# The factors of a chunked scan, queued run by run behind the splits of weights

## Chip, cores and metric

The kernel runs on one core of one Trainium2 chip. The metric is the device time of one execution in microseconds, of which the median over several runs is taken; smaller is better. A profile of one execution comes beside it, with the time at which every instruction of every engine started and ended. The engines are TensorE (PE in the profile; PEld is its weight load), VectorE (DVE), ScalarE (ACT), GpSimd (POOL) and SyncE (SP), which issues most DMAs.

## What is computed

One layer of a streaming encoder for 288 tokens: 256 of a new stream and 32 of a running one, with all values in float32. The change lies in the state-space mixer, whose scan is, per chunk:

```python
xc = (xh * dt[..., None]).reshape(b, c, q, G, J, P)
acum = jnp.cumsum(a, axis=-1)
diff = acum[..., :, None] - acum[..., None, :]
lmat = jnp.exp(jnp.where(causal, diff, -jnp.inf))
cb = jnp.einsum('bclgn,bcsgn->bcgls', Cc, Bc)
y_diag = jnp.einsum('bcgls,bcgjls,bcsgjp->bclgjp', cb, lmat, xc)
...
y_off = jnp.einsum('bclgn,bcgjpn,bcgjl->bclgjp', Cc, h_prev, jnp.exp(acum))
y = (y_diag + y_off).reshape(b, s, G, J, P) + D[..., None] * xh
```

There are 32 heads of 64 channels. Around the scan stand the projections `proj = xn @ w_in` (2048 to 5664 columns), a pooling mixer, an output projection and a feed-forward block with a depthwise convolution.

## The kernel before

**Products in three parts.** Each float32 product is made of three matmuls. A piece of weights (128 x 1024) is split: ScalarE copies it to a rounded high part `whi` (L137 in `split_w`), VectorE subtracts to get the low part `wlo` (L138), and TensorE multiplies high by high, high by low and low by high (L144 to L146). Each of `raw`, `whi` and `wlo` has four buffers. A `project` is 256 columns of an output, 16 tiles deep: four pieces, 24 matmuls each, into two accumulators `acc`.

**The mixer's loop.** After the first columns, seven projects make the channels `xs` (scan numbers 1 to 7) and eight make the gate `z` (numbers 8 to 15). Behind each project VectorE moves its two accumulators out of PSUM: for a gate that is `z = acc * rstd` (L555, twice), whose last instruction is kept in `last_in[0]`. Then `scan(i)` is called.

**The scan.** The heads are treated in eight fours, q0 to q7. `four_in(q)` loads a four's decays `gb`, its state `h0t` and its channels `xw` through SP, and makes its factors. On ScalarE that is an exponential for `ce` and one for `elast`, twelve Relu (L496) and one exponential over 128 x 1664 values of `m` (L499). On VectorE it is three products: `ce` (L489), `xw` (L492) and `m` (L501). `gb`, `h0t`, `xw`, `ce` and `m` have two buffers each. `four_out` is the use: 16 small matmuls into `py` a four (L523), then VectorE adds the result to `xs`. `four_in` is called in the scans of `SCAN_IN = {5, 6, 7, 8, 9, 11, 12, 13}`, `four_out` for the two fours that are ready in those of `SCAN_OUT = {7, 9, 12, 14}`, at its start. So the scans 7, 9, 12 and 14 let out q0 and q1, q2 and q3, q4 and q5, q6 and q7.

**The order of work.** Each engine runs its own queue in order. Where an instruction stands in a queue is set by a scheduler that works ahead of the run; the code leads it by priorities (`tc.high_priority`; the evacuations and the splits go ahead of what is written before them), by `tc.keep_in_program_order`, and by `tc.issue_after(x)`, which puts an instruction in its engine's order behind `x`. In `four_in` all factors stand under `tc.issue_after(last_in[0].ins)`.

Of the kernel before, what the change touches and what calls it, by code (L numbers as in the profile page):

```python
# [10 lines left out]
AF = mybir.ActivationFunctionType  # L11
# [32 lines left out]
def body(  # L44
# [24 lines left out]
    act, dve, pool, pe, sp = nc.scalar, nc.vector, nc.gpsimd, nc.tensor, nc.sync  # L69
# [11 lines left out]
    def aux(shape, name):  # L81
        return aux_ps.tile(shape, F32, tag="aux", name=name)
# [7 lines left out]
    def halves(t):  # L90
        return t.rearrange("p (r j) -> p r j", r=2)
# [20 lines left out]
    def wtile(part, n, nc_):  # L112

        t = wpool.tile([P, 1024 + 64], F32R, tag=part, name="w" + part)
        return t[:, 58 : 58 + n * nc_].rearrange("p (k c) -> p k c", k=n)

    ahead = [0]

    def fetch_w(view, kb, nk, c0, nc_):
        raw = wpool.tile([P, nk, nc_], F32, tag="raw", name="raw")  # L120
        with tc.high_priority(offset=ahead[0]):
            sp.dma_start(out=raw, in_=view[:, c0 // 256, kb : kb + nk, :nc_])
        return raw

    def split_w(raw, kb, nk, nc_, after=()):

        out = []
        step = min(nk, 1024 // nc_)
        for k in range(0, nk, step):
            n = min(step, nk - k)  # L130
            hi = wtile("hi", n, nc_)
            lo = wtile("lo", n, nc_)
            with ExitStack() as order:
                order.enter_context(tc.high_priority(offset=ahead[0]))
                for ins in after:
                    order.enter_context(tc.issue_after(ins.ins))
                act.activation(hi, raw[:, k : k + n, :], AF.Copy)  # L137
                dve.tensor_tensor(lo, raw[:, k : k + n, :], hi.bitcast(F32), op=ALU.subtract)  # L138
            out.append([(kb + k + i, hi[:, i, :], lo[:, i, :]) for i in range(n)])
        return out  # L140
# [123 lines left out]
    for kb, n in chunks:  # L264
        raw = wpool.tile([P, n, 768], F32, tag="raw", name="raw")
# [19 lines left out]
        for k in range(kb, kb + n):  # L285
# [11 lines left out]
            hi, lo = wtile("hi", 1, 768)[:, 0, :], wtile("lo", 1, 768)[:, 0, :]  # L297
# [20 lines left out]
    for r in range(4):  # L318
        for q in range(4):
            k = 4 * q + r  # L320
# [28 lines left out]
    last_in = [None]  # L349
# [123 lines left out]
    def four_in(q):  # L473

        c = slice(2 * P * q, 2 * P * q + 2 * P)
        gb = mp.tile([P, 4, MW], F32, tag="gb", bufs=2, name="gb")
        sp.dma_start(out=gb, in_=g_d[4 * q : 4 * q + 4, :].unsqueeze(0).broadcast_to([P, 4, MW]))
        h0t = mp.tile([P, 2 * P], F32, tag="h0t", bufs=2, name="h0t")
        sp.dma_start(out=h0t, in_=state_ssd[:, c])
        xw = mp.tile([P, 3, 2 * P], F32, tag="xw", bufs=2, name="xw")  # L480
        sp.dma_start(out=xw[:, 0:2, :], in_=xs_d[:NP_, c].rearrange("(b p) c -> p b c", p=P))
        sp.dma_start(out=xw[:, 2, :], in_=xs_d[NT - P :, c])
        ce = mp.tile([P, 4, NS], F32, tag="ce", bufs=2, name="ce")
        m = mp.tile([P, 4, MW], F32, tag="m", bufs=2, name="m")
        with tc.issue_after(last_in[0].ins):
            act.activation(ce, gb[:, :, 384:], AF.Exp)
            act.activation(elast[:, 4 * q : 4 * q + 4], gb[:, :, MW - 1], AF.Exp)
            cs = bc[2 + q // 4][:, NP_:]
            dve.tensor_tensor(ce, ce, cs.unsqueeze(1).broadcast_to([P, 4, NS]), op=ALU.mult)  # L489
            w = tok[:, :, 1, 4 * q : 4 * q + 4].unsqueeze(3).broadcast_to([P, 3, 4, 64])  # L490
            x4 = xw.rearrange("p b (r q) -> p b r q", r=4)
            dve.tensor_tensor(x4, x4, w, op=ALU.mult)  # L492
            for j in range(4):
                h = 4 * q + j
                for b, (lo_, hi_) in enumerate(((0, 256), (256, 384), (384, MW))):
                    act.activation(  # L496
                        m[:, j, lo_:hi_], gb[:, j, lo_:hi_], AF.Relu, bias=tok[:, b, 0, h : h + 1], scale=-1.0
                    )
            act.activation(m, m, AF.Exp, scale=-1.0)  # L499
            gi = q // 4  # L500
            got = dve.tensor_tensor(m, m, cbt[:, gi : gi + 1, :].broadcast_to([P, 4, MW]), op=ALU.mult)  # L501
        return xw, h0t, ce, m, got

    def four_out(q, ys, xw, h0t, ce, m, _, after=None):

        ops = []
        for k in range(4):
            for j in range(4):
                c = slice(64 * j, 64 * j + 64)
                y = ys[j // 2][64 * (j % 2) : 64 * (j % 2) + 64, :]  # L510
                if k == 0:
                    ops.append((y[:, 0:256], xw[:, 0, c], m[:, j, 0:256], True, False))
                elif k == 1:
                    ops.append((y[:, 128:256], xw[:, 1, c], m[:, j, 256:384], False, True))
                elif k == 2:
                    ops.append((y[:, 256:], xw[:, 2, c], m[:, j, 384:], True, False))
                else:
                    ops.append((y[:, 256:], h0t[:, c], ce[:, j, :], False, True))
        for y, w_, v_, go, end in ops:
            with ExitStack() as order:  # L520
                if after is not None:
                    order.enter_context(tc.issue_after(after.ins))
                ins = pe.matmul(y, w_, v_, start=go, stop=end)  # L523
            tc.keep_in_program_order(ins)
            after = None
        for i in range(2):
            t = 2 * q + i
            dve.scalar_tensor_tensor(xs[t], xs[t], dcol[:, t : t + 1], ys[i], op0=ALU.mult, op1=ALU.add)

    def gate_rstd(t, pin=False):  # L530
        p_ = aux([P, NT], "psum_g")
        ins = pe.matmul(p_, mean, gsum[t], start=True, stop=True)
        if pin:
            tc.keep_in_program_order(ins)
        o = const.tile([P, NT], F32, tag="spread", bufs=3, name="rg")
        root(o, p_, 0.5)
        return o
# [42 lines left out]
    fours = list(range(NX // 2))  # L580
    gates = list(range(NX))
    done = [-1]
    ready = []
    rg = []

    def scan(i):
        if i in SCAN_OUT:
            ys = [aux([P, NT], "py") for _ in range(3)] + [acc_ps.tile([P, NT], F32, tag="acc", name="py_a")]
            for n, (q, got) in enumerate(ready):
                four_out(q, ys[2 * n : 2 * n + 2], *got, after=None if n else ready[-1][1][-1])  # L590
            done[0] = 2 * ready[-1][0] + 1
            ready.clear()
        if i == 13:
            assert gates[0] >= 8
            rg.append(gate_rstd(0, True))
        if i in SCAN_IN:
            q = fours.pop(0)
            assert 2 * q + 1 < len(xs)
            ready.append((q, four_in(q)))

    def run_gates():
        while gates and gates[0] in zs and gates[0] <= done[0]:
# [2 lines left out]
    for i in range(1, NX // 2):  # L605
        ps = project(win, [(O_X + 256 * i, 256)], xn, K16)
        xs_evac(i, ps)
        xs_conv(i - 1)
        scan(i)
# [189 lines left out]
    def state_in(x, apart=False):  # L799

        if apart:
            room = [state_slot() for _ in range(5)]
            hi, lo = (room[3], room[4], room[0]), room[1:3]
        else:
            hi = stp[0].tile([P, 3, 512], F32R, tag="shi", name="shi")
            lo = stp[0].tile([P, 2, 512], F32R, tag="slo", name="slo")
        if apart:
            for b in (2, 0, 1):
                act.activation(hi[b], x[b], AF.Copy)
                q = top if b == 2 else slice(0, P)  # L810
                o = hi[2] if b == 2 else lo[b]
                dve.tensor_tensor(o[q], x[b][q], hi[b][q].bitcast(F32), op=ALU.subtract)
        else:
            act.activation(hi, x, AF.Copy)
            dve.tensor_tensor(hi[top, 2, :], x[top, 2, :], hi[top, 2, :].bitcast(F32), op=ALU.subtract)
            dve.tensor_tensor(lo, x[:, 0:2, :], hi[:, 0:2, :].bitcast(F32), op=ALU.subtract)
            hi, lo = ([t[:, b, :] for b in range(t.shape[1])] for t in (hi, lo))
        return hi, lo
# [41 lines left out]
    for grp in ((0, 1), (2,), (3,), (4,), (5,), (6,), (7,)):  # L860
# [5 lines left out]
        if grp[0] == 2:  # L866
            j = grp[0] // 2 - 1
            x = state_load(j)
            hi, lo = state_in(x)
# [49 lines left out]
    for k in range(KD):  # L919
        if k % 2 == 0:  # L920
            raw = wpool.tile([P, 2, 896], F32, tag="raw", name="raw")
# [4 lines left out]
        hi = act.activation(halves(a[:, 0, :]), src, AF.Copy, scale=g_ffn_pre[:, k : k + 1])  # L926
# [10 lines left out]
        else:  # L937
            q = out_temp()
# [217 lines left out]
    for kb, n in ((0, K_RUN), (K_RUN, 8), (K_RUN + 8, 8)):  # L1156
        raw = fetch_w(wd2, kb, n, (KD - 2) * P, 256)
# [141 lines left out]
```

## Time and profile before

| | |
|---|---|
| median of 3 runs | 1233.65 us (1233.14 to 1234.08) |
| profiled execution | 1235.27 us, of which the span of its instructions is 1233.0 |
| TensorE busy | 1225.3 us, 99% of the span |
| VectorE busy | 888.2 us, 72% |
| ScalarE busy | 670.2 us, 54% |
| mixer with its scan | about 86 to 240 us of the span |
| let out of the scans 7, 9, 12, 14 | about 131, 158.6, 197.7 and 226.2 us |

A row of the timeline gives the start in us, the duration, the engine, the line of the code, the operation with what it writes and reads, and in brackets an idle time ahead of it with what ended that. A row of groups gives the count, the busy time, the mean length in ns, and the idle time ahead with its releaser. A row of waits tells which instruction waited for which: microseconds in all, times, longest. In windows each row is a stretch of time with the busy time of each engine, the granted clock of TensorE (1.00 is full), the busy share of the DMA engines and the GB/s.

### The profile page before, as it was taken

How to read it: one execution, taken by the hardware profiler on the slowest of the kernel's cores; microseconds unless marked ns; L12 is line 12 of the kernel's file. 1: busy time of each engine (PE TensorE's matmuls, PEld its weight loads, DVE VectorE, ACT ScalarE, POOL GpSimd, SP SyncE). 2: the span in 40 equal slices, each digit the busy share in tenths (PEclk: the TensorE clock that was granted, in tenths of full speed). 3: DMA queues.
4: the chain of work that ended last, by engine and by line, in shares of the span. 5: the costliest groups of instructions: out<-in, count | busy, mean ns of one | idle time of the engine just before them, and what ended most of it. 6: DMA issues, size and time to landing. Idle time of an engine off the chain costs nothing.

```text
span 1233.0 us, 25222 instructions
## 1 busy us (share of the span) xinstructions
PE 1225.3 (99%) x10059; PEld 1213.7 (98%) x10059; DVE 888.2 (72%) x1484; ACT 670.2 (54%) x1011; POOL 276.3 (22%) x427
## 2 busy tenths in 40 slices
PE   9999999999999999999999999999999999999998
PEld 9999999999999999999999999999999999999997
DVE  8899998989664599887776744446777777765555
ACT  8557787546554466645554544334555454554443
POOL 6395442131341200221211200001112121101110
PEclk9999999999999999999999999999999999999999
DMA  9668785466576555676655455555555555576763
GB/s 356 197 208 307 263 279 172 149 243 221 199 242 216 191 177 201 200 228 181 208 185 171 166 185 179 169 191 188 189 172 175 188 184 172 175 252 198 217 190 118
DMA packets 87589, 249.82 MB, mean 203 GB/s; under 512 B 45712, under 2 KB 51920, under 8 KB 65200
## 3 DMA queue, kind: packets, MB, share of 16 engines
q1 hardware_dynamic: 83184, 240.78, 58.3%
q0 software_dynamic: 3712, 6.95, 1.9%
q8 instruction: 78, 1.28, 0.4%
q10 hardware_dynamic: 576, 0.49, 0.1%
q14 instruction: 39, 0.32, 0.1%
HBM read 236.23 MB, written 11.95 MB: 201 GB/s over the span
## 4 chain that ended last, share of the span: by engine, by line
PE 63%; DMA 1%; DVE 1%; ACT 0%; issue 0%; DVEq 0%
PE acc L144 20%; PE acc L145 20%; PE acc L146 20%; DMA st<-xs_d 1%; PE acc_x L145 0%; PE acc_x L144 0%; PE acc_x L146 0%; PE run_a L1172 0%; PE low L1170 0%; PE run_b L1185 0%; DVE rm L247 0%; PE low L146 0%; PE low L145 0%; PE low L144 0%; DVE sh L836 0%; PE y_ps L1215 0%
## 5 line engine op out<-in xcount | busy, mean ns | idle before, releaser
L138 DVE TENSOR_TENSOR wlo<-raw,whi 128x1024 fp32r<-128x1024 f32 (+1 forms) x386 | 461.3, 1198 | 245.6 <-ACT whi L137 245.3
L137 ACT ACTIVATE whi<-raw 128x1024 fp32r<-128x1024 f32 (+1 forms) x386 | 396.9, 1031 | 349.2 <-PE acc L145 283.4
L145 PE MATMUL acc<-hn,whi 128*128 128x288 f32 x1360 | 382.9, 286 | 0.0
L146 PE MATMUL acc<-hn,wlo 128*128 128x288 f32 x1360 | 382.7, 286 | 0.0
L144 PE MATMUL acc<-hn,whi 128*128 128x288 f32 x1360 | 382.2, 286 | 0.3 <-ACT hn L926 0.3
L144 PEld LDWEIGHTS acc<-hn,whi 128*128 128x128 f32 x1360 | 254.2, 189 | 0.8 <-ACT hn L926 0.7
L145 PEld LDWEIGHTS acc<-hn,whi 128*128 128x128 f32 x1360 | 254.7, 189 | 0.1
L146 PEld LDWEIGHTS acc<-hn,wlo 128*128 128x128 f32 x1360 | 254.6, 189 | 0.0
L144 PE MATMUL acc<-xn,whi 128*128 128x288 f32 x686 | 197.2, 289 | 0.0
L145 PE MATMUL acc<-xn,whi 128*128 128x288 f32 x686 | 195.6, 287 | 0.0
L146 PE MATMUL acc<-xn,wlo 128*128 128x288 f32 x686 | 192.3, 287 | 0.6 <-DVE wlo L138 0.6
L144 PE MATMUL acc<-fa,whi 128*128 128x288 f32 x660 | 188.8, 286 | 0.0
L145 PE MATMUL acc<-fa,whi 128*128 128x288 f32 x660 | 188.8, 286 | 0.0
L146 PE MATMUL acc<-fa,wlo 128*128 128x288 f32 x660 | 188.8, 286 | 0.0
L980 POOL COPY fc_stage<-ebuf 128x4 f32<-128x4 f32 x88 | 28.7, 326 | 463.4 <-DVE ebuf L979 401.2
L144 PEld LDWEIGHTS acc<-xn,whi 128*128 128x128 f32 x686 | 130.1, 190 | 1.4 <-issue 0.9
L145 PEld LDWEIGHTS acc<-xn,whi 128*128 128x128 f32 x686 | 130.1, 190 | 0.3
L146 PEld LDWEIGHTS acc<-xn,wlo 128*128 128x128 f32 x686 | 128.3, 190 | 1.0 <-DVE wlo L138 1.0
L144 PEld LDWEIGHTS acc<-fa,whi 128*128 128x128 f32 x660 | 124.7, 189 | 0.0
L145 PEld LDWEIGHTS acc<-fa,whi 128*128 128x128 f32 x660 | 124.7, 189 | 0.0
L146 PEld LDWEIGHTS acc<-fa,wlo 128*128 128x128 f32 x660 | 124.7, 189 | 0.0
L984 ACT ACTIVATE fc<-ebuf,pf 128x290 f32<-128x290 f32 x88 | 54.4, 622 | 78.7 <-DVE ebuf L979 78.7
(312 smaller groups left out, 1799.8 us busy)
## 6 DMA issues: line engine op xcount, KB each, us to landing
raw<-in_w_up SPq DMA_DIRECT2D x80, 1024.0 KB, 4.8
raw<-in_w_in SPq DMA_DIRECT2D x38, 1024.0 KB, 5.1
raw<-in_w_down SPq DMA_DIRECT2D x32, 1024.0 KB, 4.8
raw<-in_w_out SPq DMA_DIRECT2D x23, 1024.0 KB, 5.1
raw<-in_w_down SPq DMA_DIRECT2D x16, 768.0 KB, 4.5
raw<-in_w_up SPq DMA_DIRECT2D x8, 896.0 KB, 4.7
gb<-g_d SPq DMA_DIRECT2D x8, 832.0 KB, 6.6
raw<-in_w_first SPq DMA_DIRECT2D x5, 768.0 KB, 8.5
```

The source lines that it names most:

```text
L137: act.activation(hi, raw[:, k : k + n, :], AF.Copy)
L138: dve.tensor_tensor(lo, raw[:, k : k + n, :], hi.bitcast(F32), op=ALU.subtract)
L144: pe.matmul(out, wh, hi, start=start, stop=False)
L145: pe.matmul(out, wh, lo, start=False, stop=False)
L146: pe.matmul(out, wl, hi, start=False, stop=stop)
L980: pool.tensor_copy(fc_stage[:, :, :, i], e[:, 256:324].rearrange("p (s c) -> p s c", c=34)[:, :, 0:2])
L984: act.activation(c, e[:, 0:290], AF.Identity, bias=pf[:, 3, i : i + 1], scale=pf[:, 0, i : i + 1])
```

## The change

`four_in` now only loads, and returns its tiles. The factors stand in a new function, `four_mul`, under one more `issue_after`: behind the split `after` of a piece of weights, taken from `splits`, the list of all splits on ScalarE so far. A queue `loads` holds the fours that are loaded, and `four_next` makes the factors of the oldest. When two are loaded, in a scan of `SCAN_IN`, the older is taken: q0 and q1 in scan 6 (behind the last split but one and the last), q2 in scan 8, q4 in 11, q6 in 13 (behind the last split). A four that is still in `loads` when a scan lets out, which is q3 in scan 9, q5 in 12 and q7 in 14, is taken there, ahead of its own use, behind the fourth split from the end.

```diff
@@ split_w
+    splits = []
...
-                act.activation(hi, raw[:, k : k + n, :], AF.Copy)
+                splits.append(act.activation(hi, raw[:, k : k + n, :], AF.Copy))
@@ four_in
-        with tc.issue_after(last_in[0].ins):
+        return gb, xw, h0t, ce, m
+
+    def four_mul(q, gb, xw, h0t, ce, m, after):
+
+        with tc.issue_after(last_in[0].ins), tc.issue_after(after.ins):
             act.activation(ce, gb[:, :, 384:], AF.Exp)
@@ scan
-    ready = []
+    loads, ready = [], []
+
+    def four_next(after):
+        q, tiles = loads.pop(0)
+        ready.append((q, four_mul(q, *tiles, after)))
 
     def scan(i):
         if i in SCAN_OUT:
+            if loads:
+                four_next(splits[-4])
...
         if i in SCAN_IN:
             q = fours.pop(0)
             assert 2 * q + 1 < len(xs)
-            ready.append((q, four_in(q)))
+            loads.append((q, four_in(q)))
+            if len(loads) == 2:
+                four_next(splits[-2 if i == 6 else -1])
+                if i == 6:
+                    four_next(splits[-1])
```

The queues of both kernels hold the same instructions: 9873 rows on TensorE, 1486 on VectorE. In the rows that follow, the line is that of its own kernel (after's are up to 15 higher), a name's number tells buffers apart, and in brackets stand the engines and DMA queues whose semaphores an instruction waits for.

ScalarE, ahead of the output of scan 9, before: the last of q3's factors (`m_2226`) runs into q2's exponential (`m_2043`), with no split of weights between them.

```order
L496 ACTIVATE m_2226<-gb_2218,tok_734 128x256
L496 ACTIVATE m_2226<-gb_2218,tok_734 128x128
L499 ACTIVATE m_2043<-m_2043 128x1664
L496 ACTIVATE m_2226<-gb_2218,tok_734 128x32
L137 ACTIVATE whi_2261<-raw_2259 128x1024
```

The same place in the changed kernel; q3's `m` is now `m_2208`, its `ce` is `ce_2207`, and `whi_2243` is the same piece of weights as `whi_2261`.

```order
L501 ACTIVATE m_2043<-gb_2035,tok_734 128x32
L504 ACTIVATE m_2043<-m_2043 128x1664
L377 ACTIVATE tanh_1765<-conv_1760 128x291
L138 ACTIVATE whi_2243<-raw_2241 128x1024
L491 ACTIVATE ce_2207<-gb_2200 128x128
L492 ACTIVATE elast_825<-gb_2200 128x4
L501 ACTIVATE m_2208<-gb_2200,tok_734 128x256
```

A split stands between the two runs now. On VectorE, before, q3's products stand right behind the `z` of project 8 (`z_2182`), a whole project ahead of their use:

```order
261 L555 TENSOR_TENSOR z_2182<-acc_2063,rstd_124 128x288 [waits PE_49]
262 L489 TENSOR_TENSOR ce_2225<-ce_2225,bc_772 128x128
263 L492 TENSOR_TENSOR xw_2222<-xw_2222,tok_734 128x768 [waits DMAHW6_49,DMAHW4_49]
264 L501 TENSOR_TENSOR m_2226<-m_2226,cbt_795 128x1664 [waits Activation_49]
265 L138 TENSOR_TENSOR wlo_2320<-raw_2317,whi_2319 128x1024 [waits Activation_49]
```

In the changed kernel q2's products stand there, and q3's 20 rows later, behind the second `z` of project 9 (`z_2359`, whose accumulator `acc_2240` takes the last matmuls before the output of scan 9):

```order
275 L139 TENSOR_TENSOR wlo_2505<-raw_2502,whi_2504 128x1024 [waits DMAHW6_49,PE_49,Activation_49]
276 L560 TENSOR_TENSOR z_2357<-acc_2239,rstd_124 128x288 [waits PE_49]
277 L373 SCALAR_TENSOR_TENSOR conv_2168<-ebuf0_110,pah_122,conv_2168 128x291 [waits DVE_49]
278 L181 STREAM_TRANSPOSE blocks_1989<-xs_1978 128x288 [waits DMASW2_49,DMASW1_49,DMASW3_49,DMASW0_49,DVE_49]
279 L373 SCALAR_TENSOR_TENSOR conv_2185<-ebuf1_112,pah_122,conv_2185 128x291 [waits Activation_49,Pool_49]
280 L560 TENSOR_TENSOR z_2359<-acc_2240,rstd_124 128x288 [waits PE_49]
281 L494 TENSOR_TENSOR ce_2207<-ce_2207,bc_772 128x128
282 L497 TENSOR_TENSOR xw_2204<-xw_2204,tok_734 128x768 [waits DMAHW5_49,DMAHW3_49]
283 L506 TENSOR_TENSOR m_2208<-m_2208,cbt_795 128x1664
284 L139 TENSOR_TENSOR wlo_2509<-raw_2502,whi_2508 128x1024 [waits Activation_49]
```

q5 and q7 stand in the same way behind the `z` of projects 12 and 14. On TensorE, in the output of scan 9, the end of q2's block and the beginning of q3's, before:

```order
L523 MATMUL py_2379<-ce_2042,h0t_2037 64x32 [waits DMAHW1_49]
L523 MATMUL py_2379<-ce_2042,h0t_2037 64x32
L523 MATMUL py_2380<-ce_2042,h0t_2037 64x32 x2
L523 MATMUL py_2381<-m_2226,xw_2222 64x256 [waits DMAHW4_49,PE_49]
L523 MATMUL py_2381<-m_2226,xw_2222 64x256
```

and in the changed kernel:

```order
L528 MATMUL py_2379<-ce_2042,h0t_2037 64x32 [waits DMAHW1_49]
L528 MATMUL py_2379<-ce_2042,h0t_2037 64x32
L528 MATMUL py_2380<-ce_2042,h0t_2037 64x32 x2
L528 MATMUL py_2381<-m_2208,xw_2204 64x256 [waits DMAHW3_49,DVE_49,PE_49]
L528 MATMUL py_2381<-m_2208,xw_2204 64x256
```

The order of the matmuls is the same; the first of q3's block has a wait for VectorE (`DVE_49`) more. The first matmuls of q5's and q7's blocks gain the same wait; those of q1's do not.

## Prediction

> **What bounds the kernel now.** I read the top of the page first, then the waits of TensorE, then its busy time by stage over the stretch in which the change works.
>
> ```profile
> span 1233.0 us, 25222 instructions
> PE 1225.3 (99%) x10059; PEld 1213.7 (98%) x10059; DVE 888.2 (72%) x1484; ACT 670.2 (54%) x1011; POOL 276.3 (22%) x427
> ```
>
> ```profile
> PE acc L146 <- DVE wlo L138: 0.6, 2, 0.4
> ```
>
> ```profile
> 130.00:160.00 30.00, 29.80 (x283) 28.38 (x283) 28.85 (x52) 23.46 (x48) 10.46 (x20) 1.00 0.83 288
> 160.00:195.00 35.00, 35.00 (x317) 34.67 (x314) 33.09 (x55) 27.05 (x58) 16.02 (x23) 1.00 0.69 237
> 195.00:225.00 30.00, 29.62 (x272) 28.52 (x271) 24.12 (x33) 25.33 (x48) 3.95 (x3) 1.00 0.57 191
> ```
>
> The columns of the last fence are the stretch, its length, then the busy time of PE, PEld, DVE, ACT and POOL, the granted clock, the DMA share and GB/s. TensorE is the bound everywhere: whatever makes it wait lengthens the run by the wait, and nothing else does. In the scan it idles 0.20 + 0.38 us, which are the two waits for a `wlo` in the middle row. VectorE is nearly as full between 130 and 160 (28.85 of 30), so its order of work matters there; ScalarE has room (23.46 of 30).
>
> The pieces that are moved, grouped over the scan (count | busy us, mean ns | idle before):
>
> ```profile
> L137 ACT ACTIVATE whi<-raw 128x1024 fp32r<-128x1024 f32 x47 | 48.6, 1046 | 4.6 <-PE acc L145 4.4 <-ACT whi L137 0.2
> L496 ACT ACTIVATE m<-gb,tok 128x256 f32<-128x256 f32 (+2 forms) x96 | 31.0, 398 | 0.3 <-PE py L523 0.3
> L499 ACT ACTIVATE m<-m 128x1664 f32<-128x1664 f32 x8 | 12.6, 1578 | 0.0
> L501 DVE TENSOR_TENSOR m<-m,cbt 128x1664 f32<-128x1664 f32 x8 | 15.1, 1888 | 7.9 <-ACT m L499 7.9
> L146 PE MATMUL acc<-xn,wlo 128*128 128x288 f32 x369 | 104.7, 287 | 0.6 <-DVE wlo L138 0.6
> ```
>
> One four of heads is (31.0 + 12.6) / 8 = 5.5 us on ScalarE. TensorE's pace in its stream is 1233.0 / 10059 = 0.123 us a matmul, so a piece of weights (24 matmuls) feeds it for 2.94 us and a project (96) for 11.8 us.
>
> **The change, part by part.** *Counts.* Nothing is added or removed, and TensorE's order of matmuls is the same in both kernels: cost nil. *The loads.* On SP's queue they move by a place or two; they are needed later than before, so their landing stays covered by at least the project that now lies between load and factors. That cover gone, a late one would hold ScalarE's run, and then the product of it, not TensorE directly. Cost nil.
>
> *ScalarE's runs, one behind each split.* Before, two runs could stand in a row between two splits:
>
> ```profile
> 132.05 1.04 ACT L137 ACTIVATE whi<-raw 128x1024 fp32r<-128x1024 f32 x1
> 140.75 1.58 ACT L499 ACTIVATE m<-m 128x1664 f32<-128x1664 f32 x1
> 142.44 1.05 ACT L137 ACTIVATE whi<-raw 128x1024 fp32r<-128x1024 f32 x1
> ```
>
> That is 10.4 us from split to split, 3.5 pieces, against up to four pieces held in buffers. With one run (5.5 us) between two splits the distance is under two pieces. What this can give back is what TensorE lost to `wlo`: 0.6 us of waiting, and for each of the two waits at most 0.287 − 0.123 = 0.16 us, since a matmul that starts alone takes its whole length: 0.9 us in all, bounds 0 and 0.9. I take 0.9, because in the new order neither of the two `wlo` stands directly behind the product that delayed it.
>
> *VectorE's products.* This is the term that decides. For q3, q5 and q7 the change queues `ce`, `xw` and `m` behind the evacuation `z` of the very project whose end releases their own py block; before, they stood behind the `z` of the project ahead. The queues ahead show it for q3, and TensorE's py rows gain a wait for VectorE that they did not have. Before, in the trace, the same place on VectorE:
>
> ```profile
> 148.47 0.45 DVE L555 TENSOR_TENSOR z<-acc,rstd 128x288 f32<-128x288 f32 x1
> 148.84 0.28 DVE L489 TENSOR_TENSOR ce<-ce,bc 128x128 f32<-128x128 f32 x1
> 149.04 0.95 DVE L492 TENSOR_TENSOR xw<-xw,tok 128x768 f32<-128x768 f32 x1
> 149.91 1.88 DVE L501 TENSOR_TENSOR m<-m,cbt 128x1664 f32<-128x1664 f32 x1
> 151.71 1.22 DVE L138 TENSOR_TENSOR wlo<-raw,whi 128x1024 fp32r<-128x1024 f32 x1
> ...
> 160.71 0.45 DVE L555 TENSOR_TENSOR z<-acc,rstd 128x288 f32<-128x288 f32 x1
> 161.07 0.42 DVE L377 SCALAR_TENSOR_TENSOR xs<-tanh,conv 128x256 f32<-128x256 f32 x1
> ```
>
> and on TensorE:
>
> ```profile
> 158.35 0.29 PE L146 MATMUL acc<-xn,wlo 128*128 128x288 f32 x1
> 158.57 1.73 PE L523 MATMUL py<-m,xw 128*64 128x256 f32 x24
> ...
> 160.36 0.41 PE L523 MATMUL py<-m,xw 128*64 128x256 f32 x2
> ```
>
> From the start of the last `z` to the end of `m` is 0.37 + 0.20 + 0.87 (starts to starts) + 1.88 = 3.32 us. The project's last matmul ends at 158.64, and the second four's py block starts at 160.36: a cover of 1.72 us, which is the first four's block. A semaphore's pass costs 0.03 us from ScalarE to VectorE, by these rows (140.75 + 1.58 = 142.33 above):
>
> ```profile
> 142.36 1.89 DVE L501 TENSOR_TENSOR m<-m,cbt 128x1664 f32<-128x1664 f32 x1 [1.12 <-ACT m L499]
> ```
>
> I take 0.04, as an estimate from it, for each pass to and from TensorE. So even with VectorE idle at the project's end, TensorE waits 3.32 − 1.72 + 0.08 = 1.7 us: the floor of each of the three new waits. What comes on top is VectorE's lateness at `z`.
>
> *Out of scan 9 (q2, q3).* Here VectorE is a full queue: from the `z` at 148.47 to the `z` at 160.71 its rows follow without a gap. In the new order the rows between the same two (product of q2, four `wlo`, five conv, two pairs of xs, two transposes, one `z`) sum to 11.9 us in these durations, so `z` comes at 160.4 and `m` is done at 163.7; TensorE, without the removed wait of 0.4 before it, would be there at 160.0: a wait of 3.8. It is shorter if VectorE reaches the first of the two earlier than 148.47, by 1.5 us at most (TensorE's earlier project ended at 158.64 − 11.8 = 146.9). Bounds 1.7 and, with `z` at before's own 160.71, 160.71 + 3.32 + 0.05 − 160.0 = 4.1. I take 3.5, near the row of the full queue.
>
> *Out of scan 12 (q4, q5) and 14 (q6, q7).* Before's rows there:
>
> ```profile
> 197.49 0.29 PE L146 MATMUL acc<-xn,wlo 128*128 128x288 f32 x1
> 197.70 1.72 PE L523 MATMUL py<-m,xw 128*64 128x256 f32 x24
> 199.49 0.63 PE L523 MATMUL py<-m,xw 128*64 128x256 f32 x4
> ...
> 225.99 0.29 PE L146 MATMUL acc<-xn,wlo 128*128 128x288 f32 x1
> ...
> 228.00 0.63 PE L523 MATMUL py<-m,xw 128*64 128x256 f32 x4
> ```
>
> ```profile
> 198.68 1.37 DVE L138 TENSOR_TENSOR wlo<-raw,whi 128x1024 fp32r<-128x1024 f32 x1 [0.38 <-ACT whi L137]
> 199.97 0.44 DVE L555 TENSOR_TENSOR z<-acc,rstd 128x288 f32<-128x288 f32 x1
> ...
> 229.17 0.81 DVE L555 TENSOR_TENSOR z<-acc,rstd 128x288 f32<-128x288 f32 x2
> ```
>
> The second `z` starts one step of 0.37 later, at 200.34 and 229.54, 2.6 and 3.3 us behind the projects' last matmuls (197.78 and 226.28). If VectorE stays as late as that, `m` ends at 203.7 and 232.9 and the waits are 4.2 and 4.9 us: the upper bounds. But by then one product (2.9 us) that stood ahead of these `z` stands behind them, and the wait at the first place has let VectorE catch up; 2.6 − 2.9 is below nothing and 3.3 − 2.9 is 0.4. So both are nearest the floor. I add 0.4 to each, at 198.68 for the `whi` that `wlo` waited for: 2.1 and 2.1.
>
> *Who is late next.* VectorE's `wlo`, queued behind each product, are needed by the project behind it; its first two pieces are split before the `z`, so TensorE has 5.9 us of work when it goes on. No further wait there. After 250 us the orders are those of before, so nothing is given back.
>
> **Sum:** 3.5 + 2.1 + 2.1 − 0.9 = +6.8 us. Against the profiled execution (1235.27, span 1233.0) that is 1242.1; that one was 1.6 above the median of the runs, 1233.65, and the forecast for the median is **1240.4 us**. About 0.2%, 2.5 us, is what a measurement can tell from no change.
>
> **Rivals.** *A clock drop in the longest wait.* TensorE runs at full clock throughout, but at the start its matmuls came at half pace for the first microseconds, and at the end the grant fell after work had ended:
>
> ```profile
> 7.29 0.45 PE L144 MATMUL acc<-xn,whi 128*128 128x288 f32 x1
> 7.53 0.45 PE L145 MATMUL acc<-xn,whi 128*128 128x288 f32 x1
> ...
> 9.06 0.29 PE L144 MATMUL acc<-xn,whi 128*128 128x288 f32 x1
> ```
>
> ```profile
> 1227.52 1.13 PE L1215 MATMUL y_ps<-ft,diag 128*128 128x512 f32 x2 [0.60 <-ACT diag L1214]
> ```
>
> ```profile
> 1230.00:1231.00 1.00, 0.00 (x0) 0.00 (x0) 0.00 (x0) 0.00 (x0) 0.00 (x0) 0.94 0.91 340
> 1231.00:1232.00 1.00, 0.00 (x0) 0.00 (x0) 0.00 (x0) 0.00 (x0) 0.00 (x0) 0.50 0.55 209
> ```
>
> The last matmul ended at 1228.65 and the grant fell near 1230.9, 2.2 us later. A wait of 3.5 us could do the same; at a step of 0.24 instead of 0.12 for the three or more microseconds seen at the start, half of them are lost: some 1.7 us more, 1242.1. [...]
>
> *VectorE as late as before at all three places:* 4.1 + 4.2 + 4.9 − 0.9 = +12.3, 1245.9. For it speaks how full VectorE is up to 195; against it the moved product.
>
> *Only floors:* 3 × 1.7 − 0.9 = +4.2, 1237.9; it needs VectorE idle at 158 too.
>
> *Not slower.* The change does what its order is for, and the products are hidden: each `m` would have to be done within the 1.72 us of the first block, which the rows contradict (`m` alone takes 1.88), unless TensorE's end of the project and the `z` lie further ahead of the block than I read. Then only the gain counts: 1232.7. It decides at three waits under 0.3 us each. With waits of about 1 us the result would lie within 0.2%.
>
> **How the numbers follow.** Three waits without a clock drop: 0.53 (own range 1238.3 to 1242.3). Clock drop: 0.22. As late as before: 0.10. Floors: 0.08. Hidden, or nearly so: 0.07, of which 0.05 lie within 0.2% (0.9 us is 0.08%) and 0.02 are kept for a gain beyond it. Slower by over 0.2% is the rest, 0.93. The range, 1237.2 to 1244.8, leaves out the hidden case and the dearest part of the late one.
>
> **What would show it.** Right: TensorE's waits gain `py` waiting for VectorE's `m`, three times, together 6 to 9 us, the first the longest, and lose `acc` waiting for `wlo`; in each, `ce`, `xw`, `m` follow the second `z`. Wrong: py waits under 1 us, new waits for `wlo` or `whi` (a split starved behind a run), or a granted clock under 1.00 near 163 us.

## Result and the profile after

The changed kernel took 1242.26 us (median of 4 runs, 1241.59 to 1243.31) against 1233.39 for the kernel before beside it (4 runs): a ratio of 1.0070, with a 95% interval of 1.0057 to 1.0083. It is 8.9 us slower, where 6.8 were forecast; the time lies in the range of 1237.2 to 1244.8. The profiled execution took 1242.37 us, its span is 1240.4.

The top of the page, and TensorE's waits of the changed kernel:

```profile
span 1240.4 us, 25219 instructions
PE 1226.3 (99%) x10059; PEld 1214.9 (98%) x10059; DVE 886.6 (71%) x1484; ACT 670.9 (54%) x1011; POOL 274.9 (22%) x427
...
PE py L528 <- issue: 5.3, 2, 3.7
PE py L528 <- DVE m L506: 1.5, 1, 1.5
...
PE acc L147 <- DVE wlo L139: 0.6, 2, 0.5
```

Busy times are the same as before to about 1 us on TensorE; three waits at `py` of 6.8 us together are new. Two of them are put down to "issue", which means that the profile shows no releaser; the rows of both engines show it. A four's block is 32 small matmuls, 24 with `m` and 8 with `ce`. Scan 9 on TensorE, first q2's block and then the start of q3's, and the same stretch on VectorE:

```profile
157.60 1.73 PE L528 MATMUL py<-m,xw 128*64 128x256 f32 x24
159.16 0.40 PE L528 MATMUL py<-ce,h0t 128*64 128x32 f32 x8
163.31 1.12 PE L528 MATMUL py<-m,xw 128*64 128x256 f32 x4 [3.75 <-issue]
...
166.87 0.61 PE L145 MATMUL acc<-xn,whi 128*128 128x288 f32 x1
167.27 0.45 PE L146 MATMUL acc<-xn,whi 128*128 128x288 f32 x1
```

```profile
159.89 0.46 DVE L560 TENSOR_TENSOR z<-acc,rstd 128x288 f32<-128x288 f32 x1
160.26 0.29 DVE L494 TENSOR_TENSOR ce<-ce,bc 128x128 f32<-128x128 f32 x1
160.46 0.96 DVE L497 TENSOR_TENSOR xw<-xw,tok 128x768 f32<-128x768 f32 x1
161.32 1.89 DVE L506 TENSOR_TENSOR m<-m,cbt 128x1664 f32<-128x1664 f32 x1
163.13 1.22 DVE L139 TENSOR_TENSOR wlo<-raw,whi 128x1024 fp32r<-128x1024 f32 x1
```

`z`, `ce`, `xw`, `m`, without a gap: 3.32 us from the start of `z` to the end of `m` at 163.21, and TensorE goes on at 163.31. Scans 12 and 14:

```profile
206.73 0.65 PE L528 MATMUL py<-m,xw 128*64 128x256 f32 x4 [1.53 <-DVE m L506]
...
236.35 0.65 PE L528 MATMUL py<-m,xw 128*64 128x256 f32 x4 [1.58 <-issue]
```

In scan 9 q3's block takes its first four matmuls in 1.12 us where scan 12's take 0.65, and the project behind runs at 0.24 us a matmul. The granted clock (the number ahead of the last two in each row) says why:

```profile
160.00:161.00 1.00, 0.00 (x0) 0.00 (x0) 1.00 (x3) 0.00 (x0) 0.47 (x1) 1.00 0.94 377
161.00:162.00 1.00, 0.00 (x0) 0.00 (x0) 1.00 (x2) 0.00 (x0) 0.50 (x1) 0.95 1.06 362
162.00:163.00 1.00, 0.00 (x0) 0.00 (x0) 1.00 (x1) 0.00 (x0) 1.00 (x3) 0.50 0.88 253
...
168.00:169.00 1.00, 1.00 (x7) 1.00 (x7) 1.00 (x5) 0.46 (x2) 1.00 (x3) 0.63 0.99 379
169.00:170.00 1.00, 1.00 (x11) 1.00 (x10) 1.00 (x4) 0.72 (x2) 1.00 (x2) 1.00 1.05 365
```

Half clock lasts from 161.9 to 168.7. TensorE's matmuls stand in the same order in both kernels, so the start of the same matmul can be compared one by one. The table gives how much later than in the kernel before it started, counted from 115 us on (so that the first microseconds of an execution, which differ between executions by up to 2 us, are left out):

| lateness in us at (time in before) | 136 | 156 | 171 | 211 | 227 | 247 | 371 | 395 | end |
|---|---|---|---|---|---|---|---|---|---|
| changed | 1.16 | 0.69 | 7.20 | 8.92 | 8.27 | 10.04 | 10.03 | 10.03 | 9.07 |
| changed, second profile | 1.16 | 0.70 | 6.08 | 7.81 | 7.16 | 8.93 | 8.93 | 9.32 | 8.70 |
| changed, third profile | 1.16 | 0.69 | 6.22 | 7.95 | 7.30 | 9.06 | 9.06 | 9.06 | 8.11 |
| products behind a split's low part | 1.15 | 0.69 | 0.69 | 0.69 | 0.04 | 0.04 | 0.04 | 0.04 | 0.33 |
| only q3, q5, q7 late | 0.00 | −0.47 | 5.85 | 7.58 | 6.93 | 8.69 | 8.69 | 9.02 | 8.08 |
| scan 9's wait filled | 1.16 | 0.69 | 4.58 | 8.38 | 7.72 | 9.49 | 9.49 | 10.98 | 10.03 |
| all three waits filled | 1.16 | 0.70 | 4.58 | 6.78 | 6.13 | 7.85 | 7.85 | 10.63 | 9.68 |
| all three filled, second profile | 1.16 | 0.69 | 4.58 | 6.77 | 6.12 | 7.84 | 7.84 | 9.97 | 9.29 |
| q0 and q1 as before | 0.00 | −0.47 | 6.42 | 8.14 | 7.49 | 9.26 | 9.26 | 9.26 | 8.96 |
| low part, and q1 too | 0.61 | 0.14 | 0.14 | 0.14 | −0.51 | −0.51 | −0.51 | −0.27 | −1.22 |
| low part, q0 and q1 as before | 0.00 | −0.47 | −0.47 | −0.40 | −1.05 | −1.05 | −1.05 | −0.32 | −1.27 |

The first row, step by step: +1.16 before scan 7, −0.47 (the first removed wait), +6.5 in scan 9, +1.72 in scan 12, −0.65 (the second removed wait), +1.77 in scan 14. Of scan 9's 6.5 the wait is 3.9 and the half clock 2.6: in the kernels whose wait is filled with other matmuls (below) the clock stays full there, and their step, 4.58 − 0.69, is the wait alone. A step is a little more than the wait in it (1.72 against 1.53 in scan 12, 1.77 against 1.58 in scan 14), since matmuls in a stream overlap (one starts every 0.12 us and takes 0.29) and the first behind a wait doesn't. Most of the step of −0.96 near 440 us is a wait (`psum_m`, 0.5 us) that the profiled execution of the kernel before had and this one had not.

### The profile page after: what moved, and what is told of

Its sections match the earlier page's. It is cut to its first block, busy times and chain, and to the rows that moved or that the text cites. A ratio compares the mean times of both kernels' runs of the same rounds, so it can differ in the third digit from the quotient of the medians.

```text
span 1240.4 us, 25219 instructions
## 1 busy us (share of the span) xinstructions
PE 1226.3 (99%) x10059; PEld 1214.9 (98%) x10059; DVE 886.6 (71%) x1484; ACT 670.9 (54%) x1011; POOL 274.9 (22%) x427
## 4 chain that ended last, share of the span: by engine, by line
PE 96%; DVE 1%; DMA 1%; issue 1%; ACT 1%; SPq 0%; DVEq 0%; ACTq 0%
PE acc L145 30%; PE acc L147 30%; PE acc L146 30%; DMA raw<-in_w_first 1%; PE py L528 1%; PE acc_x L145 1%; PE acc_x L147 1%; PE acc_x L146 1%; PE py_a L528 0%; PE run_a L1187 0%; PE low L1185 0%; PE run_b L1200 0%; ACT whi L301 0%; DVE m L506 0%; DVE wlo L139 0%
```

## Experiments

**The products behind the low part of a split.** ScalarE's runs stay behind the splits where the change put them; on VectorE the products of q3, q5 and q7 are queued behind the `wlo` of the project's last split, not behind its second `z`.

```diff
-    splits = []
+    splits, lows = [], []
...
-                dve.tensor_tensor(lo, raw[:, k : k + n, :], hi.bitcast(F32), op=ALU.subtract)
+                lows.append(dve.tensor_tensor(lo, raw[:, k : k + n, :], hi.bitcast(F32), op=ALU.subtract))
...
-    def four_mul(q, gb, xw, h0t, ce, m, after):
+    def four_mul(q, gb, xw, h0t, ce, m, after, low=None):
...
-        with tc.issue_after(last_in[0].ins), tc.issue_after(after.ins):
+        with tc.issue_after((low or last_in[0]).ins), tc.issue_after(after.ins):
...
-                four_next(splits[-4])
+                four_next(splits[-4], lows[-1])
```

> The changed kernel, but VectorE's three products of q3, q5 and q7 are queued behind the low part of the last split of the project (wlo) instead of behind the second z of that project; ScalarE's runs stay where the change put them. Theory (the products stand too late on VectorE): TensorE's three waits at py (3.75 + 1.53 + 1.58 us) go, and with the longest the clock drop, which costs 2.4 us where it comes; what stays is the new wait for wlo at the split between q0's and q1's products (1.2) less the two removed waits (0.8): 1233.4 + 0.4 = 1233.8 us, and no granted clock under 1.00 near 163 us. Rival (ScalarE's runs, placed behind a split, are what makes m late): the waits stay within 1 us of those of the changed kernel, above 1239.

1233.70 us (11 runs) against 1233.74, ratio 1.0002 (0.9992 to 1.0011). No wait at `py` is left in its page of waits:

```profile
PE idle L261 <- PEq L1288: 0.8, 1, 0.8
PE psum_m L908 <- ACT msq L743: 0.8, 1, 0.8
PE acc L147 <- DVE wlo L139: 0.6, 2, 0.5
```

In scan 9, q3's `m` now ends at 155.97, five microseconds ahead of the second `z`:

```profile
154.09 1.88 DVE L506 TENSOR_TENSOR m<-m,cbt 128x1664 f32<-128x1664 f32 x1
155.89 1.21 DVE L139 TENSOR_TENSOR wlo<-raw,whi 128x1024 fp32r<-128x1024 f32 x1
...
160.52 0.81 DVE L560 TENSOR_TENSOR z<-acc,rstd 128x288 f32<-128x288 f32 x2
```

VectorE's order alone, with ScalarE's as changed, takes the whole loss back. The rival falls: the runs behind the splits cost nothing that this comparison can tell.

**Only q3, q5 and q7 late.** The kernel before with this part of the change alone, written as an edit of the changed kernel.

```diff
-        with tc.issue_after(last_in[0].ins), tc.issue_after(after.ins):
+        with tc.issue_after(last_in[0].ins), tc.issue_after((after or last_in[0]).ins):
...
             loads.append((q, four_in(q)))
-            if len(loads) == 2:
-                four_next(splits[-2 if i == 6 else -1])
-                if i == 6:
-                    four_next(splits[-1])
+            if i in (5, 6, 7, 9, 12):
+                four_next(None)
```

> The kernel before with one part of the change: only q3, q5 and q7 get their factors in the scan of their output; q0, q1, q2, q4 and q6 get theirs when they are loaded. Theory: the three waits at py alone make the loss: 1233.4 + 7.3 = 1240.7 us without a clock drop, 1243 with it; less up to 0.8 if the two removed waits for wlo go with it. Rival (the even fours and the splits that part the runs cost as much): under 1237.

1241.40 us (5 runs), ratio 1.0073 (1.0059 to 1.0086). Its row of the table shows both waits of the kernel before gone, no new one before scan 7, and nearly the same steps at scans 9, 12 and 14: 6.3, 1.73 and 1.76. In scan 9 its wait is longer (4.67 us) and its half clock shorter (3.4 us). This part alone is sufficient for the loss.

**Scan 9's wait filled.** 24 matmuls without use stand between q2's and q3's blocks.

```diff
             for n, (q, got) in enumerate(ready):
+                if n and i == 9:
+                    for _ in range(24):
+                        tc.keep_in_program_order(
+                            pe.matmul(ys[2], xn[0][:, 0, :P], xn[0][:, 1, :], start=True, stop=True)
+                        )
                 four_out(q, ys[2 * n : 2 * n + 2], *got, after=None if n else ready[-1][1][-1])
```

> The changed kernel with 24 matmuls of no use (about 2.9 us at the pace of the stream) between q2's and q3's blocks in the output of scan 9, into an accumulator that q3's block starts anew. They fill most of the wait of 3.75 us and end before m is ready. Theory (the granted clock falls because TensorE idles there, and that costs 2.4 us on top of the wait): clock 1.00 throughout, the next project starts at the same 163.3 us but at full pace, 1242.3 - 2.4 = 1239.9 us. Rival (the clock does not fall in most timed runs, or falls for another reason): 1242.3 within 0.5, or more if the fill delays q3's block.

1243.04 us (5 runs), ratio 1.0081 (1.0067 to 1.0095): the 2.4 us didn't come. TensorE's rows show the fill in the place of the wait, 0.30 us of waiting left, and full pace after it; but the clock fell in scan 12, after a wait of 2.01 us, so that the step there is 3.8 us in place of 1.72, and 1.5 us more went at 388 us:

```profile
159.31 3.47 PE L604 MATMUL py<-xn 128*128 128x288 f32 x24
163.07 0.65 PE L528 MATMUL py<-m,xw 128*64 128x256 f32 x4 [0.30 <-DVE m L506]
...
204.40 0.65 PE L528 MATMUL py<-m,xw 128*64 128x256 f32 x4 [2.01 <-DVE m L506]
```

```profile
205.00:206.00 1.00, 1.00 (x20) 0.86 (x16) 1.00 (x2) 1.00 (x5) 0.00 (x0) 0.85 0.25 87
206.00:207.00 1.00, 1.00 (x18) 0.94 (x16) 1.00 (x4) 0.97 (x2) 0.00 (x0) 0.50 0.50 74
```

**q0 and q1 as before.** Their factors are made when they are loaded; the rest is as changed.

```diff
-            if len(loads) == 2:
-                four_next(splits[-2 if i == 6 else -1])
-                if i == 6:
-                    four_next(splits[-1])
+            if i < 7:
+                four_next(last_in[0])
+            elif len(loads) == 2:
+                four_next(splits[-1])
```

> The changed kernel with the factors of q0 and q1 made when they are loaded, as before; all the rest as changed. Theory (q0's and q1's products stand back to back on VectorE with one wlo between them and hold up the splits of project 7): TensorE's waits for wlo near 124 and 127 us go, 1242.3 - 1.2 = 1241.1 us, and the waits at py and the clock drop stay. Rival (those waits come from elsewhere, for instance the loads): the same 1242.3.

1243.11 us (5 runs), ratio 1.0077 (1.0065 to 1.0090). The waits for `wlo` are gone (0.00 at 136 in the table), so their cause is right, but the time isn't less, since TensorE now waits longer in scan 9:

```profile
164.47 1.12 PE L528 MATMUL py<-m,xw 128*64 128x256 f32 x4 [4.44 <-issue]
```

VectorE's time at scan 9 is set by its own full queue (busy 14.00 of the 14 us from 157 to 171), so time that TensorE wins ahead of scan 9 it waits away there: 0.7 of the 1.2 us in this execution.

**All three waits filled.** As above, with 8 matmuls more in scans 12 and 14 each, beside the changed kernel once more; both were run a second time.

```diff
-                if n and i == 9:
-                    for _ in range(24):
+                if n and i > 7:
+                    for _ in range(24 if i == 9 else 8):
```

> The changed kernel itself once more, to stand beside the next kernel on the same chip. Theory of a clock drop that depends on where the waits fall: its runs differ by a few us with their mean granted clock (0.996 where it stays low for 6.5 us, 0.998 for about 3), 1241.5 to 1244. Rival (the drop comes in each run alike): all runs within 1 us and one mean clock.

> The changed kernel with matmuls of no use in all three waits: 24 ahead of q3's block in scan 9, 8 ahead of q5's and of q7's in scans 12 and 14, so that TensorE idles nowhere for over 0.8 us or so. Theory (idle stretches drop the granted clock, in scan 9 or, once that one is filled, in scan 12 as the fill of one wait showed): clock 1.00 from 10 us to the end, mean clock 0.999 in all runs, and the clock's share of the loss goes: 2.4 us less than the changed kernel beside it, about 1240. Rival (what the clock lost is lost anyway, because VectorE's queue is behind and would then make TensorE wait for wlo): clock 1.00, new waits for wlo, and the same time as the changed kernel within 0.5 us.

> The kernel with all three waits filled, once more, because its medians could not show what its trace showed: up to 228 us it lay 2.1 us ahead of the changed kernel (both counted from the same full-clock start), and then lost 2.5 us at 388 us to a late landing of sx<-xs_d, which lands 7.1 to 9.2 us after its issue in all kernels. Theory (the clock's share is real, the late landing is chance): again clock 1.00 and no half-clock stretch, median 1.5 to 2.5 us under the changed kernel beside it. Rival (TensorE loses at that landing whatever it gained earlier): sx lands over 8 us after its issue again, and the medians are the same within 0.7.

> The changed kernel, beside the filled one on the same chip. Theory: three waits at py of about 3.8, 1.5 and 1.6 us, a half-clock stretch of 3 to 7 us after the first, median 1242 to 1243.5. Rival: as in the expectation of the filled kernel, the same median as there within 0.7.

Changed: 1243.26 (6 runs), then 1243.04 (6 runs); filled: 1243.91 (5), then 1242.61 (6). The medians are equal within what they can tell: the 1.5 to 2.5 us forecast for the fill didn't come, as the rivals had it. The changed kernel's 12 runs here went from 1241.1 to 1247.2 us with mean clocks of 0.996 to 0.998; ten of the filled kernel's 11 have 0.999 or 1.000. The filled kernel's profiles have no half-clock stretch behind the start, and at 247 us it lay 1.1 to 2.2 us ahead of the changed one. Then it lost 2.1 to 2.8 us at one place, 388 us, where `wlo` stands on VectorE behind a product that waits for a load `sx`. In the first filled profile:

```profile
PE acc L147 <- DVE wlo L139: 3.1, 3, 2.5
PE py L528 <- DVE m L506: 1.3, 3, 0.7
```

```profile
387.02 1.76 DVE L803 TENSOR_TENSOR sx<-sx,tokd 128x1536 f32<-128x1536 f32 x1 [7.97 <-DMA sx<-xs_d]
388.69 4.63 DVE L139 TENSOR_TENSOR wlo<-raw,whi 128x1024 fp32r<-128x1024 f32 x4
```

In the three profiles with a fill this product starts 8.2 to 9.2 us after the load's last transfer was issued, in the nine others 6.8 to 8.3. This is not chance alone. The load of `sx` before this one already came late: its product starts 5.0 to 5.3 us after the last transfer was issued in all three, 3.6 to 4.2 us in the nine others. Set against TensorE's work, the last load is then issued 1.4 to 1.6 us later than in the kernel before, against 0.2 to 0.6 in the other eight. So part of this loss comes with the fill, and the filled kernel isn't the changed one with nothing but a full clock; ScalarE's rows too stand in another order in it. What in the fill makes the loads late isn't shown. What stands: the half clock costs 1.5 to 2.6 us where it falls, in all three profiles of the changed kernel; that the time at the end would be so much less without it isn't shown.

**Versions without a late product.** First, q0 and q1 one after the other too (`four_next(splits[-1])` for q0 in scan 6, and q1 in scan 7 behind the low part, ahead of its output); then the low part with q0 and q1 as before. Against the first experiment's kernel:

```diff
@@ q1 behind the low part too
-                four_next(splits[-2 if i == 6 else -1])
-                if i == 6:
-                    four_next(splits[-1])
+                four_next(splits[-1])
@@ q0 and q1 as before
-            if len(loads) == 2:
-                four_next(splits[-2 if i == 6 else -1])
-                if i == 6:
-                    four_next(splits[-1])
+            if i < 7:
+                four_next(last_in[0])
+            elif len(loads) == 2:
+                four_next(splits[-1])
```

> The first kernel's order for q3, q5 and q7 (products behind the low part of a split of the same project), and q1's product too: behind the low part of project 7's last split instead of back to back with q0's. Theory (nothing is left to wait for): no wait at py, the waits for wlo of q0's and q1's products (0.63) go, and the two of the kernel before (0.6) stay away: before - 0.9 = 1232.8 us, within what a comparison can tell. Rival (q1's product comes too late for its block in scan 7, as q3's did): a new wait at py near 130 us of 0.5 to 3 us, 1234 to 1236.

> As the kernel with the products of q3, q5 and q7 behind a split's low part, but q0 and q1 get their factors when they are loaded, as before. Theory: the waits for wlo near 124 and 127 us go and no other comes: before - 0.9 = 1232.8 us. Rival (VectorE, 96% busy from 130 to 160 us, only hands that time on to a later wait, as with q0 and q1 undone alone, where the wait in scan 9 grew from 3.75 to 4.4): a wait for wlo or py of 0.5 to 1 us between 145 and 165 us, 1233.7.

1232.79 (11 runs) and 1232.85 us (11 runs) against 1234.08 (23 runs), ratios 0.9994 (0.9985 to 1.0003) and 0.9992 (0.9984 to 1.0001). They lie 1.3 and 1.2 us under the kernel before beside them, where 0.9 was forecast, but neither interval leaves out 1. At 247 us the table has them 0.5 and 1.05 us ahead of the kernel before. That is what the idea of the change can give here, and it is at the edge of what can be measured.

## Why the prediction was right, and where not

- *The three new waits: right.* Taken 3.5, 2.1 and 2.1 us; measured as steps 3.9, 1.72 and 1.77, as waits 3.75, 1.53 and 1.58. The floor of 1.7, from 3.32 us of VectorE's rows against 1.72 of cover, is what scans 12 and 14 show. There VectorE had caught up, as the prediction said it could; in scan 14 it even waited for the project's end:

```profile
232.93 0.46 DVE L560 TENSOR_TENSOR z<-acc,rstd 128x288 f32<-128x288 f32 x1 [0.17 <-PE acc L147]
...
234.37 1.89 DVE L506 TENSOR_TENSOR m<-m,cbt 128x1664 f32<-128x1664 f32 x1
```

  The 0.4 added to each for a late `whi` wasn't paid: in scan 12 `wlo` still waits 0.38 us for it (at 201.59), but ends before the project does. In scan 9 the full queue set the wait, nearer the 3.8 worked out than the 3.5 taken.
- *The removed waits: right, and under-priced.* 0.9 taken as the most, 0.47 + 0.65 = 1.1 measured: each costs 0.27 us more than its wait, not 0.16. The working's "under two pieces" from split to split leaves out the split itself and the other rows between: in the changed kernel the splits around the runs of q2 and q3 start at 130.22, 137.79 and 143.51, which is 2.6 and 1.9 pieces.
- *A term that was put at nothing: q0 and q1.* "No further wait there" holds behind the products of q3, q5 and q7. But the change also sets q0's and q1's products behind one another in scan 6, with one `wlo` between. The prediction had looked at ScalarE's distance between splits, and at VectorE only for q3, q5 and q7:

```profile
120.06 1.89 DVE L506 TENSOR_TENSOR m<-m,cbt 128x1664 f32<-128x1664 f32 x1
121.86 0.29 DVE L494 TENSOR_TENSOR ce<-ce,bc 128x128 f32<-128x128 f32 x1
122.06 0.96 DVE L497 TENSOR_TENSOR xw<-xw,tok 128x768 f32<-128x768 f32 x1
122.93 1.22 DVE L139 TENSOR_TENSOR wlo<-raw,whi 128x1024 fp32r<-128x1024 f32 x1
...
124.50 1.89 DVE L506 TENSOR_TENSOR m<-m,cbt 128x1664 f32<-128x1664 f32 x1
126.31 1.23 DVE L139 TENSOR_TENSOR wlo<-raw,whi 128x1024 fp32r<-128x1024 f32 x1
```

```profile
124.21 0.39 PE L147 MATMUL acc<-xn,wlo 128*128 128x288 f32 x1 [0.46 <-DVE wlo L139]
127.58 0.39 PE L147 MATMUL acc<-xn,wlo 128*128 128x288 f32 x1 [0.17 <-DVE wlo L139]
```

  TensorE waits for these two `wlo` 0.63 us, a step of 1.16. It put back what the removal gave; in the kernel without it (q0 and q1 as before) scan 9's wait grew by 0.7.
- *The clock drop: the wrong one of two cases was called likeliest.* It had a chance of 0.22 and fell in all three profiled executions, at 1.5 to 2.6 us against 1.7 taken. The other executions agree: all 16 of the changed kernel have a mean clock of 0.996 to 0.998, and of 49 executions of the kernel before, beside the experiments, 48 have 0.999 or 1.000. The chance was the author's estimate: no run shows it, and the profile of the kernel before shows a fall only behind its last matmul. The runs show a fall at every wait of scan 9 that was left unfilled, five of 3.75 to 4.67 us, and one behind a wait of 2.01 us in scan 12 (last section).
- *How the parts add up.* Waits alone, by the steps to 247 us, are 7.4 us (3.9 + 1.72 + 1.77 + 1.16 − 1.12), where the sum had 6.8; with the half clock 8.9 to 10.0. The median's 8.9 fits the second better; the filled kernels, which have no half clock and the same time, keep that from being shown. That 1242.26 lies just inside the range given for three waits without a clock drop (1238.3 to 1242.3) is luck, since the drop came. Of the prediction's own signs of being wrong, two turned up: new waits for `wlo`, and a granted clock under 1.00 near 163 us. The third, `py` waits under 1 us, did not, and the three waits, 6.9 us together, are the sign of being right.

## To carry to other kernels

Before a product is queued "just ahead of its use", add up on its engine what stands between the release and its end, and set that against the work that the waiting engine still has at that moment: here 3.3 us against 1.7, and a place some eight rows earlier in VectorE's queue was worth the whole loss. An order constraint that an older instruction carries (behind the last evacuation) changes its meaning when the call is moved; read where the row lands on every engine, not only on the one the change speaks of. Where an engine is the bound and another is nearly full, time won ahead of the full one can be waited away at it, as 0.7 of 1.2 us were here.

## What was not expected of the hardware

The granted clock fell at no fixed distance from the wait. In three executions of the same kernel it was at half from 161.9 to 168.7, from 163.2 to 166.6 and from 164.9 to 168.3; the last began 0.9 us after TensorE had gone back to work at 164.01:

```profile
164.00:165.00 1.00, 0.99 (x10) 0.83 (x12) 1.00 (x2) 0.00 (x0) 0.00 (x0) 0.94 0.44 69
165.00:166.00 1.00, 1.00 (x16) 1.00 (x13) 1.00 (x4) 0.45 (x1) 0.19 (x1) 0.50 0.00 0
```

Half clock lasted 6.8 us in the first of them and 3.4 in the other two. The steps in scan 9 differ with it: 6.51, 5.38 and 5.53 us by the table, of which the wait is 3.9, so that the half clock's part is 2.6, 1.5 and 1.6. The falls at these waits, one in each of six profiles:

| kernel | TensorE's wait, us | granted clock at half |
|---|---|---|
| changed | 3.75 in scan 9 | 161.9 to 168.7 |
| changed, second profile | 3.8 in scan 9 | 163.2 to 166.6 |
| changed, third profile | 3.75 in scan 9 | 164.9 to 168.3 |
| only q3, q5, q7 late | 4.67 in scan 9 | 162.8 to 166.2 |
| q0 and q1 as before | 4.44 in scan 9 | 162.4 to 169.3 |
| scan 9's wait filled | 2.01 in scan 12 | 205.7 to 209.1 |

The longest of these waits, 4.67 us, has 3.4 us of half clock behind it, and one of 3.75 us has 6.8. Nor does the length of a wait alone tell whether the clock falls here. None followed the waits of 1.53 us in scan 12 and 1.58 us in scan 14 of the changed kernel:

```profile
205.00:210.00 5.00, 3.47 (x51) 3.03 (x48) 5.00 (x8) 4.97 (x15) 0.00 (x0) 1.00 0.68 187
235.00:240.00 5.00, 3.65 (x46) 3.46 (x47) 5.00 (x10) 0.00 (x0) 0.00 (x0) 1.00 0.09 16
```

And none followed a wait of 2.5 us near 388 us with all three waits filled (first profile), though it is longer than the 2.01 us that a fall did follow:

```profile
385.00:390.00 5.00, 2.49 (x22) 2.27 (x20) 2.98 (x3) 1.30 (x2) 0.00 (x0) 1.00 0.24 93
390.00:395.00 5.00, 5.00 (x41) 5.00 (x42) 4.38 (x4) 1.56 (x3) 0.00 (x0) 1.00 0.59 198
```

What else decides when the clock falls, and for how long, isn't shown by these runs.
